# A decoder step on one core: phases that prepare the next phase's first steps, another order of the first weight pair, layer norms split in two parts, and weight splits moved to GpSimd

## Chip, cores and metric

One core of one Trainium2 chip. The metric is device time in microseconds (us) of one execution; the kernel before has a median of 2907.46 us in three runs (2906.56 to 2908.3). PE is TensorE (matmuls), DVE is VectorE, ACT is ScalarE, POOL is GpSimd, and SP is SyncE, whose queue issues most of the DMAs.

## The reference

Two layers on 1024 prompt tokens and 64 sample tokens, width 1024, all in fp32. Each sublayer is followed by a layer norm of a scaled residual:

```python
for i in range(DEPTH):                      # DEPTH = 2
    if i % 2 == 0:                          # layer 0: gated short convolution
        gb, gc, h = split(x @ w_conv_in, 3); u = gc * h
        m = (gb * conv3(u, state)) @ w_conv_out
    else:                                   # layer 1: differential attention
        q, k, v = split(x @ w_qkv, 3)       # rotated q and k; paged cache for the samples
        a = softmax(q1 k1) - lam * softmax(q2 k2)
        m = (norm(a @ v) * subln_g * (1 - lam_init)) @ w_attn_out
    x = layernorm(ALPHA * x + m, ln_mix_g[i], ln_mix_b[i])
    g, up = split(x @ w_ffn_in[i], 2)       # FFN width 2816
    x = layernorm(ALPHA * x + (silu(g) * up) @ w_ffn_out[i], ln_ffn_g[i], ln_ffn_b[i])
```

Outputs are `y` for prompt and samples, the convolution buffers and the new keys and values.

## The kernel before

Every fp32 product is made of three passes (high by high, high by low, low by high), so each operand is split: ACT copies it into a high part, DVE subtracts to get the low part (`split_to`). Of a 128x1024 weight tile these are `whi` and `wlo` (`load_split`, from `raw`).

The phases follow each other. An **in-phase** (`in_type`: convolution in, FFN in of both layers) multiplies pairs of weight blocks with the activations by Strassen's scheme: seven products for a pair of blocks instead of eight, over seven combinations `xh`, `xl` of the activations (class `Combos`), with weight combinations `ws` (class `Weights`). Products of pair n and n + 1 are interleaved in a fixed order (`order`); six are prepared ahead. The products (`pin`, L240) have two chunks of 272 columns, 12 matmuls of 272 columns in each. Results go to DRAM (`z_dram`, `h_dram`).

An **out-phase** (`out_type`: convolution out, attention out, FFN out) loads them back, and goes over the 8 prompt tiles of 128 tokens in three groups (`GROUPS`, tiles 0, 1, 4, then 2, 5, 6, then 3, 7). Within a group a step is one of 8 feature blocks (22 in the FFN): a load of 512 KB of weights (`raw`), of the group's activations (`hr`, split into `hh` and `hl`), in group 0 of the samples' (`hs`), and 6 matmuls for each tile (`pout`, L321), and two for the samples (`pouts`, L324). Two steps are prepared ahead; `hr`, `hh` and `hl` have two buffers each. After a group `ln_prompt` normalises each tile: two DVE passes with the residual `x`, the square sum on ACT, the reciprocal root on POOL (`rs_t`, `rs_r`), and two DVE passes for mean and gain (L357), and for the root and bias (L363). The tile is stored to `x_dram` and turned: `pair` transposes tiles q and q + 4 on PE and forms the seven combinations; `to_plain` transposes one tile for qkv. Turns of a group are done between the steps of the next one (`side`), those of the last group after it.

The scheduler orders the engines, except PE in the in-phases and in qkv and attention, where the program's order stands; SP's order is fixed in the attention.

Of the kernel before, what the change touches and what calls it, by code (L numbers as in the profile page):

```python
# [9 lines left out]
F32 = mybir.dt.float32  # L10
# [32 lines left out]
GROUPS = ((0, 1, 4), (2, 5, 6), (3, 7))  # L43
# [5 lines left out]
def decoder_kernel(ctx: ExitStack, tc: tile.TileContext, i_: dict, o_: dict):  # L49
# [5 lines left out]
    wsp = ctx.enter_context(tc.tile_pool(name="wsp", bufs=8))  # L55
    sml = ctx.enter_context(tc.tile_pool(name="sml", bufs=4))
    drp = ctx.enter_context(tc.tile_pool(name="drp", bufs=1, space=bass.MemoryType.DRAM))
# [4 lines left out]
    pairs = cst.tile([P, P], F32, name="pairs")  # L62
    xsT = cst.tile([P, KT, NS], F32, name="xsT")
# [15 lines left out]
    def load_split(src, width=D, eng=None, sub=None, lo_raw=False):  # L79
        raw = rawp.tile([P, width], F32, name="raw", tag="raw")  # L80
        (eng or SP).dma_start(raw, src)
        hi = wsp.tile([P, width], F32R, name="whi", tag="w")
        lp, tag = (rawp, "raw") if lo_raw else (wsp, "w")
        lo = lp.tile([P, width], F32R, name="wlo", tag=tag)
        split_to(hi, lo, raw, sub)
        return hi, lo, raw
# [17 lines left out]
    class Combos:  # L104
# [11 lines left out]
        def pair(self, psum, x1, x2, q):  # L116

            cs = slice(32 + q * P, 32 + q * P + P)

            def turned(k0):  # L120
                ps = psum.tile([P, 2, 512], F32, name="ptr", tag="b")
                for n, x in enumerate((x1, x2)):
                    for k in range(4):
                        PE.transpose(ps[:, n, k * P:k * P + P], x[:, (k0 + k) * P:(k0 + k + 1) * P], ident)
                return ps

            def v(t):
                return t.rearrange("p (k t) -> p k t", k=4)

            def scratch(name):  # L130
                return scp.tile([P, 512], F32, name=name, tag="sc")

            ps = turned(0)
            t1, t3 = scratch("t1"), scratch("t3")
            self.put(B11, cs, v(ps[:, 0, :]))
            ACT.copy(t3, ps[:, 1, :])
            DVE.tensor_tensor(t1, t3, ps[:, 0, :], op=ALU.subtract)
            ps = turned(4)
            t2 = scratch("t2")
            DVE.tensor_tensor(t2, ps[:, 1, :], t1, op=ALU.subtract)  # L140
            DVE.tensor_tensor(t3, ps[:, 1, :], t3, op=ALU.subtract)
            self.put(B21, cs, ps.rearrange("p n (k t) -> p n k t", k=4), 2)
            self.put(X1, cs, v(t1))
            self.put(X3, cs, v(t3))
            t4 = scratch("t4")
            DVE.tensor_tensor(t4, ps[:, 0, :], t2, op=ALU.subtract)
            self.put(X2, cs, v(t2))
            self.put(X4, cs, v(t4))
# [22 lines left out]
    class Weights:  # L171


        def __init__(self, src1, src2):
            self.src = src1, src2
            self.done = {}

        def raw(self, n):
            if n not in self.done:
                t = rawp.tile([P, D], F32, name="raw", tag="raw")  # L180
                SP.dma_start(t, self.src[n])
                self.done[n] = t
            return self.done[n]

        def make(self, p):
# [23 lines left out]
            split_to(w[:, 0, :], w[:, 1, :], src)  # L209
# [6 lines left out]
    def in_type(psum, x, work):  # L216


        order = [(0, 1), (0, 2)]
        for n in range(len(work)):  # L220
            order += [(n, 7), (n, 6)] + ([(n + 1, 1)] if n + 1 < len(work) else []) + [(n, 5)]
            order += ([(n + 1, 2)] if n + 1 < len(work) else []) + [(n, 4), (n, 3)]
        made, nxt = {}, 0
        banks = {}

        def prep(upto):
            nonlocal nxt
            while nxt < min(upto, len(order)):
                n, p = order[nxt]
                made[n, p] = work[n][0].make(p)  # L230
                nxt += 1

        def mm(ps, w, p, start, chunks=(0, 1)):
            for c in chunks:
                cs = slice(c * CW, c * CW + CW)
                for k in range(4):
                    ks = slice(k * P, k * P + P)
                    b = OPERAND[p]
# [4 lines left out]
        prep(6)  # L243
        with tc.manual_schedule(engines={mybir.EngineType.PE}):
            for at, (n, p) in enumerate(order):
                put = work[n][1]
                w = made.pop((n, p))
                if p in (1, 2, 7):
                    banks[n, p] = psum.tile([P, 2, 512], F32, name=f"pin{p}", tag="b")
                ps = banks[n, {1: 1, 6: 1, 5: 1, 3: 1, 7: 7, 4: 7, 2: 2}[p]]  # L250
                mm(ps, w, p, p in (1, 2, 7))
                v = ps[:, :, :CW]
                if p in (1, 6, 5):
                    ACT.copy(put.dst({1: 0, 6: 2, 5: 3}[p]), v)
                if p in (2, 5, 4):
                    blk = {2: 0, 5: 3, 4: 2}[p]
                    d = put.dst(blk)
                    DVE.tensor_tensor(d, d, banks[n, 7][:, :, :CW] if p == 5 else v, op=ALU.add)
                    put.done(blk)
                elif p == 3:  # L260
                    put.last(v)
                prep(at + 7)


    def out_type(psum, pool, nf, h_src, s_src, w_src, res, res_s, ln):

        gb = [pool.tile([P, D], F32, name=f"ln{nm}", tag=f"ln{nm}", bufs=1) for nm in "gb"]
        for t, nm in zip(gb, ("ln_g", "ln_b")):
            SP.dma_start(t, i_[nm][ln["n"]:ln["n"] + 1, :].partition_broadcast(P))
        steps = [(g, f) for g in range(len(GROUPS)) for f in range(nf)]  # L270
        made, nxt = {}, 0

        def prep(upto):
            nonlocal nxt
            while nxt < min(upto, len(steps)):
                g, f = steps[nxt]
                nxt += 1
                w = load_split(w_src[f])
                ts = GROUPS[g]
                raw = pool.tile([P, len(ts), P], F32, name="hr", tag="hr", bufs=2)  # L280
                n = 0
                while n < len(ts):
# [4 lines left out]
                    SP.dma_start(raw[:, n:m, :], h_src[f][:, c0:c0 + (m - n) * P].rearrange("p (n t) -> p n t", t=P))  # L287
                    n = m
                hh = pool.tile([P, len(ts), P], F32R, name="hh", tag="hh", bufs=2)
                hl = pool.tile([P, len(ts), P], F32R, name="hl", tag="hl", bufs=2)  # L290
                split_to(hh, hl, raw)
                hs = None
                if g == 0:
                    if s_src is None:
                        hs = pool.tile([P, 2, 32], F32, name="hs", tag="hs", bufs=2)
                        SP.dma_start(hs, h_src[f].rearrange("p (a t) -> p a t", a=2)[:, :, 0:32])
                        hs = hs.rearrange("p a t -> p (a t)")
                    else:
                        hs = s_src(f)
                made[g, f] = w, hh, hl, hs  # L300

        side = []
        kept = {}
        prep(2)
        for g, ts in enumerate(GROUPS):
            last = g == len(GROUPS) - 1
            pss = [psum.tile([P, 2, 512], F32, name="pout", tag="b") for _ in ts]
            if g == 0:
                pq = psum.tile([P, 2, 512], F32, name="pouts", tag="b")
                xs = pool.tile([P, 512], F32, name="xs", tag="xs", bufs=1)  # L310
                fold(lambda half: xs[half * NS:half * NS + NS, :], res_s)
            for t in ts:
                kept[t] = pool.tile([P, D], F32, name="x", tag="x", bufs=3)
                SP.dma_start(kept[t], res(t))
            for f in range(nf):
                (wh, wl, raw), hh, hl, hs = made.pop((g, f))
                for n, ps in enumerate(pss):
                    for hf in range(2):
                        cs = slice(hf * 512, hf * 512 + 512)
                        for m, (a, b) in enumerate(passes(hh[:, n, :], hl[:, n, :], wh[:, cs], wl[:, cs])):  # L320
                            PE.matmul(ps[:, hf, :], a, b, start=(f == 0 and m == 0), stop=(f == nf - 1 and m == 2))  # L321
                if g == 0:
                    for half in range(2):
                        PE.matmul(pq[half * NS:half * NS + NS, 0, :], hs, raw[:, half * 512:half * 512 + 512],  # L324
                                  start=(f == 0), stop=(f == nf - 1), skip_group_check=True)
                prep(g * nf + f + 3)
                if f >= 2 and side:
                    side.pop(0)()
            while side:
                side.pop(0)()  # L330
            if g == 0:
                ss = sml.tile([P, 1], F32, name="lsms", tag="lsms", bufs=2)
# [862 lines left out]
```

## Time and profile before

| | us |
|---|---|
| median of three runs | 2907.46 |
| profiled execution, whole | 2907.33 |
| its span, first to last instruction | 2905.6 |
| conv in, conv out | 34 to 291, to about 444 |
| FFN in, out (layer 0) | to 918, to about 1212 |
| qkv, attention, attention out | to 1600, to 1976, to about 2127 |
| FFN in, out (layer 1) | to about 2602, to 2894 |

The mean granted TensorE clock is 0.971. The stages' bounds are read from the first and the last matmul of each phase on the timeline. In a row of waits the engine, its output and its line stand first, then what it waited for, the total in us, the number of waits and the longest. In a row of a table by stretches stand the bounds and the length in us, then the busy time of each engine with its instructions, the granted clock, and the DMA's share. A group's row has its total and, in ns, the mean of one instruction.

### The profile page before, as it was taken

The numbers are of one execution on the slowest core, as the hardware profiler recorded it, in microseconds if no ns is written. First come the engines' busy times: TensorE is split into PE (matmuls) and PEld (weight loads), VectorE is DVE, ScalarE is ACT, GpSimd is POOL, SyncE is SP. The second block draws the span as 40 slices with busy tenths as digits, with TensorE's granted clock in tenths as the row PEclk, the third lists the DMA queues.
The fourth block names the chain that finished last, engine by engine and source line by source line (L and its number), as shares of the span: only waits on it lengthen the run. The fifth ranks groups of instructions, "written<-read, shape, count | busy, mean of one in ns | idle before, by whom it ended". The sixth has DMA issues, their size and how long they took to land.

```text
span 2905.6 us, 51121 instructions
## 1 busy us (share of the span) xinstructions
PE 2728.5 (94%) x20436; PEld 2364.7 (81%) x20436; DVE 1497.9 (52%) x2565; ACT 1043.0 (36%) x1921; POOL 253.4 (9%) x481
## 2 busy tenths in 40 slices
PE   6999879999998999899999999997889999989997
PEld 6999559999997677689888666665679999986676
DVE  7666476555552365522222666673775555532555
ACT  4222254333332244412122556562543333322343
POOL 0000010000000010111111232330100000000100
PEclk9999989999999999899999999998999999999999
DMA  3111652222223466775877888834622222234666
GB/s 123 67 60 62 199 182 81 75 82 72 79 73 118 139 212 202 228 260 200 278 275 254 287 299 309 288 110 144 211 77 80 73 82 75 75 100 147 203 190 191
DMA packets 187728, 454.95 MB, mean 157 GB/s; under 512 B 36545, under 2 KB 85330, under 8 KB 187490
## 3 DMA queue, kind: packets, MB, share of 16 engines
q1 hardware_dynamic: 175442, 408.88, 42.3%
q0 software_dynamic: 11904, 42.55, 4.3%
q8 instruction: 160, 2.62, 0.4%
q14 instruction: 78, 0.64, 0.1%
q10 hardware_dynamic: 144, 0.26, 0.0%
HBM read 387.44 MB, written 64.17 MB: 155 GB/s over the span
## 4 chain that ended last, share of the span: by engine, by line
PE 64%; issue 23%; DMA 5%; DVE 3%; ACT 2%; POOL 2%; SPq 1%; DVEq 0%; POOLq 0%; ACTq 0%
PE pin L240 25%; PE pout L321 14%; PE psqkv L930 10%; PE psS L995 3%; PE psO L833 3%; PE pso L1030 2%; PE psS L775 2%; PE psaT L1023 1%; PE pouts L324 1%; DMA raw<-wfo 1%; PE psq L717 1%; DMA hr<-h_dram 1%; DVE wlo L77 1%; PE psS L998 1%; DVE xl L77 0%
## 5 line engine op out<-in xcount | busy, mean ns | idle before, releaser
L240 PE MATMUL pin<-xh,ws 128*128 128x272 f32 x6272 | 1199.4, 290 | 39.6 <-ACT ws L76 18.6
L240 PEld LDWEIGHTS pin<-xh,ws 128*128 128x128 f32 x6272 | 1000.3, 190 | 43.4 <-ACT ws L76 19.1
L240 PE MATMUL pin<-xl,ws 128*128 128x272 f32 x3136 | 914.2, 292 | 2.2 <-DVE xl L77 2.1
L240 PEld LDWEIGHTS pin<-xl,ws 128*128 128x128 f32 x3136 | 594.6, 190 | 3.1 <-DVE xl L77 3.1
L321 PE MATMUL pout<-whi,hh 128*128 128x512 f32 x960 | 391.4, 409 | 56.6 <-ACT hh L76 43.6
L77 DVE TENSOR_TENSOR wlo<-raw,whi 128x1024 fp32r<-128x1024 f32 x204 | 250.8, 1230 | 291.0 <-ACT whi L76 260.7
L321 PE MATMUL pout<-whi,hl 128*128 128x512 f32 x960 | 381.5, 400 | 4.2 <-DVE hl L77 4.2
L321 PE MATMUL pout<-wlo,hh 128*128 128x512 f32 x960 | 381.2, 398 | 0.0
L76 ACT CAST whi<-raw 128x1024 fp32r<-128x1024 f32 x204 | 213.6, 1048 | 287.7 <-DMA raw<-wfo 145.6
L321 PEld LDWEIGHTS pout<-whi,hh 128*128 128x128 f32 x960 | 184.3, 192 | 145.9 <-ACT hh L76 69.2
L77 DVE TENSOR_TENSOR ws<-s,ws 128x512 fp32r<-128x512 f32 x224 | 154.5, 690 | 141.6 <-ACT ws L76 141.0
L930 PE MATMUL psqkv<-whi,xTh 128*128 128x256 f32 x768 | 222.6, 290 | 2.4 <-DVE xTl L77 2.4
L321 PEld LDWEIGHTS pout<-whi,hl 128*128 128x128 f32 x960 | 183.9, 192 | 49.5 <-DVE hl L77 8.0
L321 PEld LDWEIGHTS pout<-wlo,hh 128*128 128x128 f32 x960 | 184.5, 192 | 38.2 <-DVE wlo L77 0.3
L930 PE MATMUL psqkv<-wlo,xTh 128*128 128x256 f32 x768 | 214.7, 279 | 0.0
L930 PE MATMUL psqkv<-whi,xTl 128*128 128x256 f32 x768 | 214.4, 279 | 0.0
L76 ACT CAST ws<-s 128x512 fp32r<-128x512 f32 x224 | 138.8, 620 | 205.8 <-PE pin L240 103.8
L77 DVE TENSOR_TENSOR hl<-hr,hh 128x384 fp32r<-128x384 f32 (+1 forms) x180 | 94.4, 525 | 184.0 <-ACT hh L76 183.8
L76 ACT CAST hh<-hr 128x384 fp32r<-128x384 f32 (+1 forms) x180 | 85.4, 475 | 260.8 <-PE pout L321 167.1
L94 POOL TENSOR_SCALAR rs_t<-lss 128x1 f32<-128x1 f32 x32 | 22.0, 686 | 1691.9 <-ACT pout L355 1085.7
L77 DVE TENSOR_TENSOR ws<-raw,ws 128x512 fp32r<-128x512 f32 x168 | 115.4, 688 | 99.6 <-ACT ws L76 99.6
L930 PEld LDWEIGHTS psqkv<-whi,xTh 128*128 128x128 f32 x768 | 145.0, 189 | 18.0 <-issue 14.1
(219 smaller groups left out, 3269.7 us busy)
## 6 DMA issues: line engine op xcount, KB each, us to landing
raw<-wfo SPq DMA_DIRECT2D x132, 512.0 KB, 3.9
kpg<-ck SPq DMA_DIRECT2D x128, 512.0 KB, 5.3
vpg<-cv SPq DMA_DIRECT2D x128, 512.0 KB, 4.9
raw<-wfi SPq DMA_DIRECT2D x88, 512.0 KB, 3.3
h_dram<-hf SPq DMA_DIRECT2D x44, 544.0 KB, 2.7
raw<-wci SPq DMA_DIRECT2D x24, 512.0 KB, 3.3
raw<-wco SPq DMA_DIRECT2D x24, 512.0 KB, 3.8
x_dram<-x SPq DMA_DIRECT2D x24, 512.0 KB, 3.0
```

Source lines behind the costliest of these rows:

```text
L76: ACT.copy(hi, src)
L77: (eng or DVE).tensor_tensor(lo, src, fv(hi), op=ALU.subtract)
L240: PE.matmul(ps[:, c, :CW], a, y, start=(start and k == 0 and m == 0), stop=(k == 3 and m == 2), skip_group_check=True)
L321: PE.matmul(ps[:, hf, :], a, b, start=(f == 0 and m == 0), stop=(f == nf - 1 and m == 2))
L324: PE.matmul(pq[half * NS:half * NS + NS, 0, :], hs, raw[:, half * 512:half * 512 + 512], start=(f == 0), stop=(f == nf - 1), skip_group_ch ...
L717: PE.matmul(psq[half * NS:half * NS + NS, pr * 256:pr * 256 + 256], xsT[:, 4 * kh + k, :], raws[half][:, k, :], start=(kh == 0 and k == 0) ...
L775: PE.matmul(ps[32 * t:32 * t + 32, n, :], qp[:, 2 * t + h2, :], kp[:, 2 * t + h2, :], start=(h2 == 0), stop=(h2 == 1), skip_group_check=True)
L833: PE.matmul(O[32 * t:32 * t + 32, :], PT[:, p, 32 * t:32 * t + 32], vp[:, 2 * t:2 * t + 2, :].rearrange("p h d -> p (h d)"), start=(p == 0 ...
L930: PE.matmul(ps[t][:, t % 2, :256], a[:, k, t0:t0 + P], b_[:, cs], start=(k == 0 and n == 0), stop=(k == KT - 1 and n == 2), skip_group_che ...
L995: PE.matmul(svs[c][:, bk, :], a[cp, i, :], b_[cp, bk * w:bk * w + w], start=(m == 0), stop=(m == 2), skip_group_check=True)
L998: PE.matmul(svs[c][:, nb - 1, w - P:w], idb, cmask, start=False, stop=True, skip_group_check=True)
L1030: PE.matmul(po, aT[:, k, :], vn[:, k, :], start=(k == 0), stop=(k == i))
```

## The change

The in-phase and the out-phase become classes whose steps can be prepared from outside.

1. `InPhase`: the first pair runs chunk 0 of its seven products, then chunk 1. `tail` holds the last two half-turns of the phase before, done within chunk 0. When its own products are all prepared it prepares the first two steps of the out-phase (`after`), and `fill` puts two of three products of the out-phase's first step between its last products. Eight products are prepared ahead, with 7 buffers instead of 8 for the splits.
2. `OutPhase`: one `hr` buffer and one for `hs`. Groups are `PAIRED` for convolution and attention (three `hr` loads a step in groups 0 and 1), `PLAIN` for the FFN (one, two and one). In the last group the last two features of tile 0 come first, then its norm, then those of tile 1; turns begin at the fourth feature, two per step; and the FFN's first weights are prepared.
3. `ln_prompt` with `gb` None (after convolution and attention) does one DVE pass instead of two, without gain and bias. These come in at two places: in `pair`, where ACT scales each transposed 128x128 block, 16 per pair, and in the FFN's out-phase, where POOL multiplies and adds to each reloaded residual tile.
4. Low parts of the convolution's and the attention's output weights, and of the first pair of weights of convolution and of each FFN, are subtracted on POOL, 512 columns at a time.
5. `to_plain` turns in halves, and the last two turns are done in qkv's first block. The samples' transposed activations go to `a_dram`, the first two steps of the attention's out-phase are prepared before the last heads are done, and the start loads the input in smaller pieces, and the first weights by ACT's queue.

```diff
-GROUPS = ((0, 1, 4), (2, 5, 6), (3, 7))
+PAIRED = ((0, 4, 1), (5, 2, 6), (3, 7))
+PLAIN = ((0, 1, 2), (3, 4, 5), (6, 7))
...
-    wsp = ctx.enter_context(tc.tile_pool(name="wsp", bufs=8))
+    wsp = ctx.enter_context(tc.tile_pool(name="wsp", bufs=7))
@@ load_split @@
+        if sub is POOL:
+            ACT.copy(hi, raw)
+            for cs in (slice(0, width // 2), slice(width // 2, width)):
+                POOL.tensor_tensor(lo[:, cs], raw[:, cs], fv(hi[:, cs]), op=ALU.subtract)
@@ Combos.pair(self, psum, x1, x2, q, gb) @@
+                    for k in range(4):
+                        PE.transpose(ps[:, n, k * P:k * P + P], x[:, (k0 + k) * P:(k0 + k + 1) * P], ident)
+                    for k in range(4):
+                        ACT.activation(b[:, k, :], ps[:, n, k * P:k * P + P], AF.Identity,
+                                       scale=gb[:, 0, k0 + k:k0 + k + 1], bias=gb[:, 1, k0 + k:k0 + k + 1])
+            b11, b12 = turned(0)
+            self.put(B11, cs, b11)
+            DVE.tensor_tensor(b11, b12, b11, op=ALU.subtract)
+            yield
...
@@ InPhase @@
+            first = (1, 2, 7, 6, 5, 4, 3)
+            self.steps = [(0, p, (0,)) for p in first] + [(0, p, (1,)) for p in (1, 2)]
...
+        def run(self, psum, after=None, tail=(), fill=()):
...
+                    if chunks == (0,) and p in (5, 3) and tail:
+                        tail.pop(0)()
+                    if n == len(self.work) - 1 and p in (5, 4) and fill:
+                        fill.pop(0)()
+                    if self.prep(live) and after and len(self.made) <= 6:
+                        after()
@@ OutPhase @@
-                raw = pool.tile([P, len(ts), P], F32, name="hr", tag="hr", bufs=2)
+                raw = hp.tile(shape, F32, name="hr", tag="hr", bufs=1)
...
+        def more(self, ahead=2):
+            if self.nxt < ahead:
+                self.prep(self.nxt + 1)
...
+        def fill(self, psum, n):
+            def go():
+                self.early[n] = psum.tile([P, 2, 512], F32, name="pout", tag="b")
+                self.products(self.early[n], 0, 0, n)
+            return go
...
+                for t in ts:
+                    kept[t] = pool.tile([P, D], F32, name="x", tag="x", bufs=4)
+                    SP.dma_start(kept[t], res(t))
+                    if gb:
+                        POOL.tensor_tensor(kept[t], kept[t], gb[ln["n"] - 1][0], op=ALU.mult)
+                        POOL.tensor_tensor(kept[t], kept[t], gb[ln["n"] - 1][1], op=ALU.add)
+                late = 2 if last else 0
+                wait = 3 if last else 1
+                for f in range(nf - late):
...
+                    self.prep(g * nf + f + 3)
+                    if last and after and f >= nf - 6:
+                        after()
+                    for _ in range(2 if last else 1):
+                        if f >= wait and side:
+                            side.pop(0)()
...
+                for n, t in enumerate(ts):
+                    for f in range(nf - late, nf):
+                        self.products(pss[n], g, f, n)
+                    ln_prompt(kept[t], pss[n], t, gb.get(ln["n"]), ln)
@@ ln_prompt @@
+        if gb is None:
+            DVE.tensor_scalar(x, x, nmu[:, 0:1], r[:, 0:1], op0=ALU.add, op1=ALU.mult)
+            SP.dma_start(ln["keep"](t), x)
+            return
@@ FeedForward @@
+        def first(self):
+            self.into.prep(min(len(self.into.made) + 1, 5))
...
+        def run(self, psum, tail):
+            self.into.run(psum, self.out.more, tail, [self.out.fill(psum, n) for n in range(2)])
@@ qkv, attention @@
+                            if first and t % 2 and late:
+                                late.pop(0)(psb, "pb")
...
+        wao.prep(2)
         for x in todo:
```

On PE, at the end of the convolution's in-phase, the out-phase's first matmuls followed the last product (`pin` is a product of the in-phase, `pout` of the out-phase). Before:

```order
L240 MATMUL pin_2650<-xh,ws 128x272 x2
L240 MATMUL pin_2650<-xl,ws 128x272
L240 MATMUL pin_2650<-xh,ws 128x272
L321 MATMUL pout<-whi,hh 128x512
L321 MATMUL pout<-wlo,hh 128x512
```

Now, some way ahead of the last product:

```order
L260 MATMUL pin_2722<-xl,ws 128x272
L260 MATMUL pin_2722<-xh,ws 128x272
L345 MATMUL pout<-whi,hh 128x512
L345 MATMUL pout<-wlo,hh 128x512
L345 MATMUL pout<-whi,hl 128x512
L345 MATMUL pout<-whi,hh 128x512
L345 MATMUL pout<-wlo,hh 128x512
L345 MATMUL pout<-whi,hl 128x512
L345 MATMUL pout<-whi,hh 128x512
L260 MATMUL pin_2924<-xh,ws 128x272
L260 MATMUL pin_2924<-xl,ws 128x272
```

Seven `pout` matmuls of the first step stand between two in-products, and six more behind the second of these.

On SP, where the FFN of layer 0 goes from its in-phase to its out-phase (`ev` is the last in-result, `raw` weights, `x` and `xs` residual tiles). Before:

```order
L461 DMA h_dram_21_104<-hf 128x1088
L269 DMA lnb<-ln_b 128x1024
L287 DMA hr<-h_dram_0_83 128x256
L287 DMA hr<-h_dram_0_83 128x128
L296 DMA hs<-h_dram_0_83 128x2x32
L287 DMA hr<-h_dram_1_84 128x256
L287 DMA hr<-h_dram_1_84 128x128
```

Now, where the `hr` rows of steps 0 to 2 stand far ahead:

```order
L359 DMA lng_9097<-ln_g 128x1024
L536 DMA h_dram_21_106<-ev 128x544
L332 DMA hs<-h_dram_1_86 128x2x32
L359 DMA lnb_9098<-ln_b 128x1024
L359 DMA lng_9101<-ln_g 128x1024
L359 DMA lnb_9102<-ln_b 128x1024
L109 DMA xs<-s_dram_161 64x512 x2
L372 DMA x<-x_dram_0_137 128x1024
L372 DMA x<-x_dram_1_138 128x1024
L372 DMA x<-x_dram_2_139 128x1024
L332 DMA hs<-h_dram_2_87 128x2x32
L84 DMA raw<-wfo 128x1024
```

The last row is the weights of step 3; two gain and bias tiles have joined what stands ahead of it.

On POOL, in the last group of the convolution's out-phase there were the norms' rows alone (`rs_t`, `rs_r`). Now:

```order
L91 TENSOR_TENSOR wlo<-raw,whi 128x512 x2
L102 TENSOR_SCALAR rs_t<-lss 128x1
L104 TENSOR_TENSOR rs_r<-rs_t,mhalf 128x1
L91 TENSOR_TENSOR wlo<-raw,whi 128x512 x2
L80 TENSOR_TENSOR ws<-raw,ws 128x512
L91 TENSOR_TENSOR wlo<-raw,whi 128x512 x2
L80 TENSOR_TENSOR ws<-raw,ws 128x512
L91 TENSOR_TENSOR wlo<-raw,whi 128x512 x2
L80 TENSOR_TENSOR ws<-s_4032,ws 128x512
L91 TENSOR_TENSOR wlo<-raw,whi 128x512 x2
L80 TENSOR_TENSOR ws<-s_4122,ws 128x512
L80 TENSOR_TENSOR ws<-s_4121,ws 128x512
```

The low parts of the output weights (`wlo`) and of the FFN's first weights (`ws`) now stand between the norms' rows, in POOL's one queue.

More of the change, by code (lines that the diff above doesn't have):

```diff
@@ L241, in mm @@
                                   stop=(k == 3 and m == 2), skip_group_check=True)
[L243 to L262, printed above, removed]
@@ L265, in out_type @@
[L265 to L279, printed above, removed]
-                raw = pool.tile([P, len(ts), P], F32, name="hr", tag="hr", bufs=2)
+        def run(self, psum, after=None, tail=(), fill=()):
+            tail, fill = list(tail), list(fill)
+            assert len(tail) in (0, 2)
+            live = 8
+            self.prep(live)
+            with tc.manual_schedule(engines={mybir.EngineType.PE}):
+                for at, (n, p, chunks) in enumerate(self.steps):
+                    put = self.work[n][1]
+                    w = self.made[n, p]
+                    if chunks != (0,):
+                        del self.made[n, p]
+                    role = self.ROLE[p]
+                    if p == role and chunks != (1,):
+                        self.banks[n, role] = psum.tile([P, 2, 512], F32, name=f"pin{p}", tag="b")
+                    ps = self.banks[n, role]
+                    self.products(ps, w, p, chunks)
+                    c = slice(chunks[0], chunks[-1] + 1)
+                    v = ps[:, c, :CW]
+                    if p in (1, 6, 5):
+                        ACT.copy(put.dst({1: 0, 6: 2, 5: 3}[p])[:, c], v)
+                    if p in (2, 5, 4):
+                        blk = {2: 0, 5: 3, 4: 2}[p]
+                        d = put.dst(blk)[:, c]
+                        DVE.tensor_tensor(d, d, self.banks[n, 7][:, c, :CW] if p == 5 else v, op=ALU.add)
+                        if chunks != (0,):
+                            put.done(blk)
+                    elif p == 3 and chunks != (0,):
+                        put.last(ps[:, :, :CW])
+                    if chunks == (0,) and p in (5, 3) and tail:
[4 more added lines that the diff above has]
+                        after()
@@ L300, in prep @@
[L300 to L321, printed above, removed]
-                if g == 0:
[L323 to L332, printed above, removed]
-                DVE.scalar_tensor_tensor(xs, xs, ALPHA, pq[:, 0, :], op0=ALU.mult, op1=ALU.add, accum_out=ss)
-                it = ln_sample(psum, xs, ss, ln)
-                next(it)
-                side += [lambda it=it: next(it, None)] * 5
-            for n, t in enumerate(ts):
-                ln_prompt(kept[t], pss[n], t, gb, ln)
-            for t in ts:
-                side += [lambda th=th: th() for th in ln["turn"](t, kept)]
-            if last:
-                while side:
-                    side.pop(0)()
@@ L381, in ln_sample @@
         ps = psum.tile([P, 2, 512], F32, name="pln", tag="b")
[L382 removed]
+        halves(ps[:, 0, 0:1], ss)
         t = sml.tile([P, 1], F32, name="lts", tag="lts", bufs=2)
@@ L517, in flat @@
+                work = []
                 def flat(t):
@@ L627, in decoder_kernel @@
         xTl = xtp_pool.tile([P, KT, NT], F32R, name="xTl")
-        keep, keeps = kept_in(1)
-        ffn_out(0, psum, 0, norm(1, to_plain(psum, xTh, xTl), plain_sample(xTh, xTl), keep, keeps))
-    scs.close()
+        with tc.tile_pool(name="fo0", bufs=2, reuse_waits="tile") as pool:
+            keep, keeps = kept_in(1)
+            late = ff.out.run(psum, pool, *kept_in(0),
+                              norm(1, to_plain(psum, xTh, xTl), plain_sample(xTh, xTl, xsT), keep, keeps))
+    ap3s = ExitStack()
     with tc.tile_pool(name="kvp", bufs=1, reuse_waits="tile") as kvp, \
@@ L1077, in decoder_kernel @@
                     turned = next(turn)
+        step(200)
+        for h in range(NH):
+            POOL.dma_start(a_dram[h].rearrange("p (a t) -> p a t", a=2)[:, :, 0:32],
+                           xsT[:, h, :].rearrange("p (a t) -> p a t", a=2))
+        wao.prep(2)
         for x in todo:
```

385 lines of the change are left out of this document (239 added, 146 removed).

## The prediction

> **What bounds the kernel now.** I read the page's first part, then what TensorE (PE) waited for, then a table of stretches.
>
> ```profile
> span 2905.6 us, 51121 instructions
> PE 2728.5 (94%) x20436; PEld 2364.7 (81%) x20436; DVE 1497.9 (52%) x2565; ACT 1043.0 (36%) x1921; POOL 253.4 (9%) x481
> ```
>
> PE is busy for 94% of the span and every other engine has room, so PE sets the time, and at most 2905.6 - 2728.5 = 177 us of idle time, plus the time in which PE runs slowly, can go without removing work. The change removes next to no matmuls. The profiled run took 2907.33 us, 1.7 more than its span; the median of the three runs is 2907.46, so one sum serves for both. About 0.2%, 6 us, is what a measurement of this kernel can tell from no change.
>
> ```profile
> PE pout L321 <- ACT hh L76: 43.6, 6, 10.9
> PE ptr L124 <- DVE x L363: 21.0, 4, 8.2
> PE pin L240 <- ACT ws L76: 18.6, 3, 17.0
> PE pin L240 <- DVE ws L77: 12.1, 4, 8.5
> PE ptr L414 <- DVE x L363: 11.3, 3, 6.4
> PE pout L321 <- DVE t L146: 10.1, 2, 5.0
> PE ptr L124 <- DVE t L137: 9.4, 4, 4.3
> ```
>
> Columns: total us, times, longest. These 26 waits hold 126 of the 177 us, and all are at seams: `hh` is the first operand of an out-phase, `x` the layer norm's end before the turns, `t` the turns' combinations, `ws` an in-phase's first weights. The next table cuts the span around those seams.
>
> ```profile
> core 0: us, PE busy (x) PEld busy (x) DVE busy (x) ACT busy (x) POOL busy (x), PEclk, DMA share, GB/s
> 290.80:340.00 49.20, 38.33 (x150) 25.77 (x149) 10.87 (x14) 8.84 (x13) 0.00 (x0) 0.86 0.58 183
> 340.00:375.00 35.00, 34.13 (x150) 25.91 (x150) 27.01 (x42) 16.65 (x25) 9.67 (x11) 1.00 0.70 219
> 375.00:450.00 75.00, 49.81 (x231) 40.16 (x229) 59.77 (x101) 36.62 (x63) 7.92 (x10) 0.82 0.47 159
> 910.00:950.00 40.00, 31.24 (x136) 23.41 (x136) 7.47 (x11) 5.76 (x10) 0.00 (x0) 0.83 0.52 166
> ...
> 1190.00:1240.00 50.00, 36.84 (x207) 32.55 (x206) 26.58 (x52) 19.16 (x25) 7.69 (x12) 0.83 0.66 210
> 1960.00:2010.00 50.00, 33.57 (x128) 22.80 (x127) 11.77 (x20) 12.65 (x28) 6.76 (x14) 0.73 0.39 129
> ...
> 2055.00:2135.00 80.00, 55.26 (x248) 44.40 (x246) 61.60 (x103) 37.78 (x66) 11.30 (x11) 0.83 0.47 155
> 2595.00:2640.00 45.00, 35.17 (x160) 25.26 (x161) 9.64 (x14) 8.00 (x12) 0.00 (x0) 0.89 0.52 163
> ```
>
> Idle time is the stretch less PE's busy time; in steady work (340 to 375) the granted clock is 1.00 and little is idle. After a gap the clock is low, and the same matmuls take longer:
>
> ```profile
> 301.99 6.86 PE pout L321 x18
> ...
> 320.55 4.33 PE pout L321 x18
> 324.88 1.01 PE pouts L324 x4
> ```
>
> So a seam costs its idle time plus about (1 - clock) of its busy time. Conv in to conv out: 10.9 + 2.5 (6.86 - 4.33) = 13.4. The turns before the first FFN: 25.2 + 0.18 x 49.8 = 34. FFN in to out, layer 0: 8.8 + 0.17 x 31.2 = 14. To qkv: 13.2 + 0.17 x 36.8 = 19.5. Attention to its projection: 16.4 + 9 = 25.5. The turns before the second FFN: 24.7 + 9.4 = 34. FFN in to out, layer 1: 9.8 + 3.9 = 13.7. Sum **154 us** at seven seams.
>
> **The change, part by part.** *Fill and early preparation (conv in to out).* Two steps of the out-phase are now prepared before the in-phase ends, and two of the first step's three products stand between the last in-products. The 10.9 us chain (last store, `hr` load, `hh`) is then needed only by the steps of the last two features. Of 13.4 I take **12** as gone (bounds 8 and 13.4: all but one slow restart, 2.5, and a load of 3.0, quoted below; or all).
>
> *Turns before the FFNs.* New: two of the three pairs of group 2 are turned beside its matmuls, the last pair inside chunk 0, which is 7 products of 12 matmuls. What it costs the other engines, from these rows:
>
> ```profile
> L77 DVE TENSOR_TENSOR wlo<-raw,whi 128x1024 fp32r<-128x1024 f32 x204 | 250.8, 1230 | 291.0 <-ACT whi L76 260.7 <-PE pin L240 14.8 <-PE psqkv L930 14.0
> L77 DVE TENSOR_TENSOR hl<-hr,hh 128x256 fp32r<-128x256 f32 x60 | 25.0, 419 | 13.7 <-ACT hh L76 13.7
> L77 DVE TENSOR_TENSOR xl<-t,xh 128x512 fp32r<-128x512 f32 x32 | 21.7, 683 | 3.1 <-ACT xh L76 2.9
> ...
> L1006 ACT ACTIVATE pexp<-psS,pnm 128x128 f32<-128x128 f32 x16 | 5.7, 362 | 8.9 <-DVE pnm L1002 8.9
> ```
>
> ```profile
> 369.33 1.24 DVE L77 TENSOR_TENSOR wlo<-raw,whi 128x1024 fp32r<-128x1024 f32 x1 [1.01 <-ACT whi L76]
> 370.49 1.66 DVE L77 TENSOR_TENSOR hl<-hr,hh 128x384 fp32r<-128x384 f32 x1
> ...
> 374.31 0.56 DVE L77 TENSOR_TENSOR hl<-hr,hh 128x384 fp32r<-128x384 f32 x1 [1.03 <-ACT hh L76]
> ```
>
> ```profile
> 369.56 2.17 POOL L388 TENSOR_TENSOR xs<-xs,gbf 128x512 f32<-128x512 f32 x1
> ```
>
> A pair now costs ACT 16 activations of 128x128, 16 x 0.36 = 5.8 us, and 7 casts (4.8, at DVE's 0.68), 21 for two pairs with 8 `whi` casts apart; just inside PE's group, which lasts 8 x 12/18 x 4.33 + 3.5 for transposes = 26.6. DVE has 11 operations per pair, 11 x 0.68 = 7.5, 15 for two, and 8 x 0.42 for `hl`: 18.4. POOL gets 16 half-row `wlo` operations and five `ws`. No row has that form; the nearest are 0.68 (DVE's own) and the last one quoted, 2.17, so 21 cost 14 to 46 us. The rows show more: POOL's began at 369.56 while DVE's `wlo` ran to 370.57, and `hl` ended at 372.15, 0.42 after POOL's. So POOL's own time is about 2.17 - 1.0 = 1.2, 25 us for 21, and while it ran, `hl` stood still. If the two engines ran freely side by side, 25 would fit into 26.6, and some 4 us would remain for the last pair. Standing still for each other they need 18.4 + 25 = 43, and 17 of the 34 remain, 18 with the last pair. I take the second: gain **16** at each of the two places (bounds 30: free; -3: POOL at 2.17). The shorter norm (one pass for two) is in the residue. In groups 0 and 1 the same splits on POOL, 2.4 us a step, lie beside 4.3 us of matmuls and cost nothing.
>
> The Trainium skill's page "SBUF — State Buffer", section "Who interferes with whom", states that a DVE instruction with two SBUF inputs and a GpSimd instruction that reads SBUF exclude each other for whole instructions. By that rule this term is the 16 above, without it 30; the rows at 370 us agree with it (1.66 for 0.56), and it speaks against moving splits to GpSimd while DVE turns pairs.
>
> *FFN in to out.* Filled in the same way, worth up to 14. But SyncE's queue now has four gain and bias tiles, `xs` and three residual tiles ahead of the weights of step 3, and the first of them waits for PE's last in-product, since the pool reuses the operands' memory. That is 7 x 512 KB + 128 KB + 512 KB of weights, 4.2 MB; at the 200 GB/s or so of the busy stretches 21 us, plus 2.3 for `whi` and `wlo`. PE has step 0's third product and two whole steps, 1.4 + 3 x 1.0 + 8.7 = 13, ahead of it. A new wait of 5 to 10 us per layer takes most of the gain: **4** each (bounds -3 and 12).
>
> *Out-phases with one `hr` buffer.* It was two. The last column is us from issue to landing:
>
> ```profile
> hr<-h_dram SPq DMA_DIRECT2D x88, 128.0 KB, 3.0
> ...
> hs<-h_dram SPq DMA_DIRECT2D x44, 32.0 KB, 2.3
> ```
>
> A load can start only when `hl` of the step before is done: 0.4 issue + 2.3 to 3.0 + 0.42 each for `hh` and `hl` = 3.5 to 4.2 us a step. PE's step is 2.9 (12/18 of 4.33) in the last group and 4.3 in the others. So the first two groups lose nothing; the last group of an FFN loses 0.6 x 20 = 12 at the short landing, less 5.8 that two prepared steps cover: **-7** in layer 0, **-5** in layer 1, where the last group no longer begins behind a norm (bounds 0, as the load may be early anyway, and 1.3 x 20 - 5.8 = -20, each). In the 8-step phases the lead covers it. POOL's 16 reload multiplies and adds per FFN (each twice L388's size, 2.4) I cost at nothing: matmuls hide them; uncovered they are 38 per FFN.
>
> *To qkv.* The last two turns move into qkv's first block, so PE needn't wait for the second norm: half of 19.5, **10** (bounds 3 and 16: the wait for `x` (11.3 in three) and its restarts). *Attention to projection:*
>
> ```profile
> 1985.25 0.79 PE L321 MATMUL pout<-whi,hh 128*128 128x512 f32 x1 [10.51 <-ACT hh L76]
> ```
>
> Seven of eight features don't need the last head and are now prepared before it is done, so this wait and its restart go: 10.5 + 2.5 = **13** (bounds 6 and 18).
>
> *Start and end.* The start gives **0**: PE's first chunk needs half the weights, but its sixth product waits for an evacuation that shares a buffer with the second chunk's input, and DVE has 44 half-size operations for 22 full ones, 22 x (2 x 0.68 - 1.23) = 3 more. Bounds -3 and 5 (7 half-size splits less ahead of PE). The end, where tile 6's norm now runs under tile 7's last matmuls, **2** (0 and 4).
>
> Sum: 12 + 16 + 16 + 4 + 4 - 7 - 5 + 10 + 13 + 0 + 2 = 65. 2907.3 - 65 = **2842 us**.
>
> **The rivals.** *A: all seams close.* If the two engines hardly meet and the weights of step 3 come in time: 154 less 4 to 5 a seam (one short restart), 120 gone, out-phases at no loss: **2787**. For it: every long wait named above is answered by an edit. Against it: the 370 us rows.
>
> *B: slower, the single `hr` buffer binds.* Its price is decided by where a load lies behind 512 KB of weights in the queues:
>
> ```profile
> 1188.41 4.82 DMA raw<-wfo
> ...
> 1196.77 4.82 DMA raw<-wfo
> ```
>
> The chain of waits in the last group already runs through weight loads every 8.4 us for three buffers, 2.8 a step, as long as PE's step. If `hr` lands in 4.8 like these, a step is 0.4 + 4.8 + 0.8 = 6.0: last groups lose 3.1 x 20 - 5.8 = 56 in each FFN, 112 in both, against 65 + 12 gained elsewhere: **2942**. It is level with before when the last groups cost 38 each, at a cycle of 5.1 us. Against it: a load-bound `hr` comes after its weights have landed, not behind them.
>
> *C: the lock reaches into the FFN out-phases.* The 32 reload operations hold a DVE split back by 1.1 (1.66 less 0.56) each in steps where DVE is just in time, and PE waits: 32 x 1.1 = 35: **2877**. The same skill section would have it so, and says that order of issue decides who blocks; no run here shows a 1024-wide GpSimd operation beside them.
>
> *D: the change doesn't do what it says:* the early preparations wait for buffers (7 split buffers for 8), and seams stay: 2905.
>
> **How the numbers follow.** Forecast 0.50, A 0.17, C 0.18, B 0.08, D 0.07. The range covers forecast, C and most of A, and widens at the slow end for the `hr` bounds (13 to 15 more in each FFN): 2782 to 2888. Faster is forecast, A and C, 0.85; same is most of D, 0.06; slower is B and a rest of D, 0.09.
>
> **What would show it.** Right: the waits of `pout` for `hh` fall from 43.6 to under 15; both turn stretches keep 15 to 20 us idle and slow, PE waiting there for `xl`, `ws` or `hl` with POOL busy; a wait for `whi` or `wlo` three steps into the FFN out-phases; steps of 3.4 to 3.6 us in their last groups, released by `hh`. Wrong: those steps at 2.8 or above 5; turn stretches without idle time; a long gap at the start; waits inside qkv.

## The result, and the profile after

The changed kernel takes 3059.89 us (median of four runs, 3053.22 to 3069.52) against 2907.22 before: a ratio of 1.0527, with a 95% interval of 1.0492 to 1.0563. It is 153 us slower, where 65 us less were forecast. The page of its profiled execution:

```profile
span 3064.3 us, 51378 instructions
...
PE 2787.6 (91%) x20468; PEld 2372.9 (77%) x20468; DVE 1490.7 (49%) x2527; ACT 1095.6 (36%) x2080; POOL 506.7 (17%) x638
```

PE's busy time rose by 59 us with only 32 more matmuls. Some 36 of the 59 us stand in the `pout` matmuls, of which there are as many as before: those of `whi` and `hh`, `whi` and `hl`, `wlo` and `hh` took 391, 382 and 381 us and now take 408, 390 and 393, with a lower granted clock in the stretches below. PE's idle time rose from 177 to 277 us. What it waited for (total, times, longest):

```profile
PE pout L345 <- ACT hh L79: 106.0, 82, 4.4
PE pout L345 <- DVE hl L80: 30.6, 29, 3.9
PE pin L260 <- ACT gc L284: 12.4, 2, 11.9
PE ptr L134 <- ACT xb L136: 11.2, 8, 1.7
...
PE pouts L385 <- DMA hs<-h_dram: 8.8, 3, 4.1
```

The wait for `hh` was six long waits at seams, 43.6 us. Now it is 82 short ones, 106 us: it has moved from the seams into the steps of the out-phases, and grown. By stretches, first two groups and last group of the FFN out-phase of layer 0, from the last product of the in-phase and divided at the last group's first matmul, before:

```profile
918.00:1142.30 224.30, 215.06 (x912) 156.34 (x913) 98.61 (x125) 74.86 (x102) 9.06 (x11) 0.98 0.61 186
1142.30:1208.00 65.70, 64.10 (x289) 51.80 (x287) 46.20 (x66) 34.70 (x50) 6.44 (x9) 1.00 0.73 228
```

and after:

```profile
936.60:1190.80 254.20, 224.38 (x908) 156.69 (x907) 113.71 (x127) 74.33 (x103) 46.87 (x25) 0.95 0.53 165
1190.80:1298.80 108.00, 74.51 (x289) 51.85 (x287) 53.09 (x68) 36.71 (x56) 16.46 (x13) 0.95 0.45 150
```

(length, PE busy, weight loads, DVE, ACT, POOL, clock, DMA share, GB/s.) Nearly the same matmuls take 30 us longer in the first two groups and 42 in the last. A step in the last group, on ACT (start, duration, tile, and the idle time before with its releaser):

```profile
1268.77 1.04 ACT L79 CAST whi<-raw 128x1024 fp32r<-128x1024 f32 x1 [3.13 <-PE pout L345]
1269.72 0.40 ACT L79 CAST hh<-hr 128x256 fp32r<-128x256 f32 x1
1273.26 1.04 ACT L79 CAST whi<-raw 128x1024 fp32r<-128x1024 f32 x1 [3.14 <-PE pout L345]
1274.21 0.40 ACT L79 CAST hh<-hr 128x256 fp32r<-128x256 f32 x1
```

on SP, and on PE:

```profile
1266.12 0.33 SPq L323 DMA_DIRECT2D hr<-h_dram  x1
1269.79 0.33 SPq L84 DMA_DIRECT2D raw<-wfo  x1
1270.61 0.33 SPq L323 DMA_DIRECT2D hr<-h_dram  x1
```

```profile
1270.17 0.51 PE L345 MATMUL pout<-whi,hh 128*128 128x512 f32 x1 [1.44 <-ACT hh L79]
1274.66 0.50 PE L345 MATMUL pout<-whi,hh 128*128 128x512 f32 x1 [1.44 <-ACT hh L79]
```

The loads of `hr` in this stretch, with their size and the time from issue to landing:

```profile
hr<-h_dram SPq DMA_DIRECT2D x2, 128.0 KB, 3.0
```

A step takes 4.49 us (1270.17 to 1274.66), of which PE waits 1.44. Two loops run here. One is the forecast's: `hr` issued 1266.12, landed 3.0 later at about 1269.1, cast as `hh`, then `hl`, then the next `hr` at 1270.61. It has some 0.6 us to spare, since `hh` begins only at 1269.72. The other goes through PE: the step's end frees a split buffer, ACT starts `whi`, and `hh`, which PE waits for, stands behind `whi` in ACT's queue. Its links fill the step: 0.95 from `whi` to `hh` (1268.77 to 1269.72), 0.45 to the first matmul, and 3.09 from there to the next `whi` (1273.26).

### The profile page after: what moved, and what is told of

It reads as the page before. It is cut to its first block, busy times and chain, and to the rows that moved or that the text cites. A ratio compares the mean times of both kernels' runs of the same rounds, so it can differ in the third digit from the quotient of the medians.

```text
span 3064.3 us, 51378 instructions
## 1 busy us (share of the span) xinstructions
PE 2787.6 (91%) x20468; PEld 2372.9 (77%) x20468; DVE 1490.7 (49%) x2527; ACT 1095.6 (36%) x2080; POOL 506.7 (17%) x638
## 5 line engine op out<-in xcount | busy, mean ns | idle before, releaser
L345 PE MATMUL pout<-whi,hh 128*128 128x512 f32 x960 | 408.1, 426 | 109.6 <-ACT hh L79 106.0
L345 PE MATMUL pout<-whi,hl 128*128 128x512 f32 x960 | 389.6, 417 | 30.9 <-DVE hl L80 30.6
L345 PE MATMUL pout<-wlo,hh 128*128 128x512 f32 x960 | 392.9, 410 | 7.1 <-DVE wlo L80 7.1
L80 DVE TENSOR_TENSOR wlo<-raw,whi 128x1024 fp32r<-128x1024 f32 x156 | 211.5, 1357 | 337.5 <-ACT whi L79 163.1
L79 ACT CAST whi<-raw 128x1024 fp32r<-128x1024 f32 x156 | 163.5, 1048 | 405.5 <-DMA raw<-wfo 197.3
L80 DVE TENSOR_TENSOR ws<-s,ws 128x512 fp32r<-128x512 f32 x212 | 146.3, 690 | 262.8 <-ACT ws L79 262.8
L80 DVE TENSOR_TENSOR hl<-hr,hh 128x384 fp32r<-128x384 f32 (+1 forms) x180 | 125.5, 697 | 205.6 <-ACT hh L79 187.9
L374 POOL TENSOR_TENSOR x<-x,lng 128x1024 f32<-128x1024 f32 x16 | 41.9, 2621 | 1032.5 <-DMA x<-x_dram 995.6
L79 ACT CAST ws<-raw 128x512 fp32r<-128x512 f32 x168 | 104.2, 621 | 294.9 <-PE pin L260 203.5
L91 POOL TENSOR_TENSOR wlo<-raw,whi 128x512 fp32r<-128x512 f32 x96 | 131.5, 1392 | 153.5 <-ACT whi L89 95.7
```

The costliest lines, as they stand in the source:

```text
L79: ACT.copy(hi, src)
L80: (eng or DVE).tensor_tensor(lo, src, fv(hi), op=ALU.subtract)
L91: POOL.tensor_tensor(lo[:, cs], raw[:, cs], fv(hi[:, cs]), op=ALU.subtract)
L374: POOL.tensor_tensor(kept[t], kept[t], gb[ln["n"] - 1][0], op=ALU.mult)
```

## The experiments

Two theories: H, the single `hr` buffer; L, GpSimd and DVE standing still for each other. Ratios are to runs of the kernel before on the same chip, with their 95% interval.

**1. Two `hr` buffers.**

```diff
-raw = hp.tile(shape, F32, name="hr", tag="hr", bufs=1)
+raw = hp.tile(shape, F32, name="hr", tag="hr", bufs=2)
```

> The changed kernel with two buffers for `hr` again, nothing else. Theory H (the single buffer makes load, `hh`, `hl` and the next load one chain, whose load lies behind 512 KB of weights): most of the loss goes, 80 to 130 us faster than the changed kernel, 2930 to 2980 us, and a step of the last group of an FFN out-phase falls from 4.5 to under 3.1 us. Theory L (GpSimd and DVE standing still for each other): less than 30 us faster, over 3030.

2916.67 us, ratio 1.0032 (1.002 to 1.0045): 143 us faster than the changed kernel, more than the 80 to 130 that H gave. The same two stretches:

```profile
917.40:1141.50 224.10, 215.01 (x907) 154.58 (x906) 113.98 (x128) 73.61 (x104) 47.09 (x25) 0.97 0.59 187
1141.50:1209.50 68.00, 65.60 (x289) 52.73 (x287) 50.32 (x68) 36.15 (x55) 13.91 (x12) 0.97 0.67 224
```

30 us come back in the first two groups and 40 in the last. On ACT in the last group:

```profile
1180.00 0.41 ACT L79 CAST hh<-hr 128x256 fp32r<-128x256 f32 x1 [1.34 <-DMA hr<-h_dram]
1180.31 1.04 ACT L79 CAST whi<-raw 128x1024 fp32r<-128x1024 f32 x1
1182.34 0.41 ACT L79 CAST hh<-hr 128x256 fp32r<-128x256 f32 x1 [0.99 <-DMA hr<-h_dram]
1182.65 1.05 ACT L79 CAST whi<-raw 128x1024 fp32r<-128x1024 f32 x1
1185.25 0.41 ACT L79 CAST hh<-hr 128x256 fp32r<-128x256 f32 x1 [1.55 <-DMA hr<-h_dram]
```

Now `hh` waits for its load and no longer behind a `whi` that waits for PE, and steps come every 2.3 to 2.9 us. The order of ACT's queue, which the scheduler writes, is another too. Counted from the phase's first casts, the `whi` at 1268.77 in the changed kernel is that of step 64 and the `hh` behind it that of step 61; here the `hh` of step 57 (1180.00) stands ahead of the `whi` of step 58. So the edit gives back a buffer and, with it, this order, and what each alone is worth was not separated. What remains is 10 us slower than before: without its worst part the change gains nothing.

**2. All splits on DVE, one `hr` buffer.**

```diff
-out = OutPhase(KT, z_dram, i_["wco"], PAIRED, POOL)
+out = OutPhase(KT, z_dram, i_["wco"], PAIRED)
...
-wao = OutPhase(KT, a_dram, i_["wao"], PAIRED, POOL)
+wao = OutPhase(KT, a_dram, i_["wao"], PAIRED)
...
-                                              sub=POOL if f == 0 else None), Put(f)) for f in range(FT)])
+                                              sub=None), Put(f)) for f in range(FT)])
```

> The changed kernel with the low parts of weights subtracted on DVE again, one `hr` buffer. Theory H: within 15 us of the changed kernel (3045 to 3075), the FFN out-phases unchanged, as they had no split on GpSimd. Theory L: 40 us or more faster (under 3020), in the stretches of the convolution's and the attention's out-phases and turns.

3027.53 us, ratio 1.0415 (1.039 to 1.044): 32 us faster, between the two (H at most 15, L at least 40).

**3. No gain and bias on reloaded tiles, one `hr` buffer.**

```diff
-                    if gb:
-                        POOL.tensor_tensor(kept[t], kept[t], gb[ln["n"] - 1][0], op=ALU.mult)
-                        POOL.tensor_tensor(kept[t], kept[t], gb[ln["n"] - 1][1], op=ALU.add)
```

> The changed kernel without the gain and bias on the reloaded residual tiles (32 GpSimd operations of 128x1024 left out; the output lacks them). Theory H: within 15 us of the changed kernel. Theory L for the FFN out-phases: 30 us or more faster, in their first two groups.

The output lacks the gain and bias. 3033.55 us in one run, 26 us faster: again between the two. So L has a part too.

**4. The kernel before with one `hr` buffer.**

```diff
-raw = pool.tile([P, len(ts), P], F32, name="hr", tag="hr", bufs=2)
+raw = pool.tile([P, len(ts), P], F32, name="hr", tag="hr", bufs=1)
```

> The kernel before with one `hr` buffer in place of two, nothing else. Theory H: 60 to 130 us slower than before (2967 to 3037), in the out-phases, steps of about 4.5 us in the last groups. Theory L: within 20 us of before.

3099.13 us in one run, 192 us slower than before: the one edit costs more than the whole change, and more than the 60 to 130 of H. On ACT in its last group:

```profile
1285.55 0.41 ACT L76 CAST hh<-hr 128x256 fp32r<-128x256 f32 x1 [1.10 <-DMA hr<-h_dram]
...
1290.42 0.41 ACT L76 CAST hh<-hr 128x256 fp32r<-128x256 f32 x1 [0.53 <-DMA hr<-h_dram]
```

These two casts are 4.87 us apart, and both waited for their load. At other steps of this group `hh` stands right behind a `whi` that waited for PE, as in the changed kernel; on average a step takes 5.7 us (124.8 us for 22).

**5. Two `hr` buffers and all splits on DVE** (1 and 2 together).

> The changed kernel with two `hr` buffers and all low parts of weights subtracted on DVE again. If GpSimd and DVE stand still for each other at the turns (theory L, beside H), 15 to 35 us faster than with two `hr` buffers alone (2880 to 2902), in conv out, attention out and their turns; if moving the splits cost nothing once the loads are early, within 6 us of it (2911 to 2923).

2898.41 us, ratio 0.9971 (0.9958 to 0.9983): 18 us faster than experiment 1, as L gives. Rows by operation; the turns' low parts (total, mean in ns of one) in experiment 1:

```profile
L80 DVE TENSOR_TENSOR xl<-xb,xh 128x512 fp32r<-128x512 f32 x56 | 49.0, 890 | 20.4 <-ACT xh L79 19.9
```

and here:

```profile
L80 DVE TENSOR_TENSOR xl<-xb,xh 128x512 fp32r<-128x512 f32 x56 | 37.5, 686 | 11.2 <-ACT xh L79 10.8
...
L424 DVE TENSOR_SCALAR x<-x,nmu,rs_r 128x1024 f32<-128x1024 f32 x16 | 13.0, 814 | 11.5 <-POOL rs_r L104 10.1 <-ACT whi L79 0.7 <-ACT hh L79 0.7
```

Each low part takes 204 ns less where GpSimd has no splits. The second row, the shorter norm's pass, is read at the end.

**6. The `hr` load ahead of the weight load, one buffer.** The line `w = load_split(...)` of `prep` stands behind the `hr` loads.

> The changed kernel with one `hr` buffer, and the `hr` load issued ahead of the step's weight load instead of behind it. If the load's place behind 512 KB of weights makes the cycle long, a last group's step falls from 4.5 to about 3.6 us (0.4 + 2.1 to 2.3 + 0.8) and the kernel to 2990 to 3030; if the chain through one buffer is long in itself, it stays within 15 us of the changed kernel.

3075.02 us in one run: 15 us slower, neither of the two. ACT in its last group:

```profile
1254.47 1.04 ACT L79 CAST whi<-raw 128x1024 fp32r<-128x1024 f32 x1 [3.11 <-PE pout L345]
1255.42 0.40 ACT L79 CAST hh<-hr 128x256 fp32r<-128x256 f32 x1
1258.95 1.04 ACT L79 CAST whi<-raw 128x1024 fp32r<-128x1024 f32 x1 [3.13 <-PE pout L345]
1259.90 0.40 ACT L79 CAST hh<-hr 128x256 fp32r<-128x256 f32 x1
1264.76 0.40 ACT L79 CAST hh<-hr 128x256 fp32r<-128x256 f32 x1 [4.46 <-DMA hr<-h_dram]
```

Most steps of the group are like the first two shown: 4.48 us, with `hh` right behind a `whi` that waited for PE. A few, like the last, wait for their load. So the place behind 512 KB of weights isn't what makes the step long. What the load's loop would take without the other stays open; an eighth split buffer, which would loosen the loop through PE, was not tried.

**7. Half of the block operations on DVE** (on experiment 5).

```diff
+                        if n == 0:
                             ACT.activation(b[:, k, :], ps[:, n, k * P:k * P + P], AF.Identity, ...)
+                        else:
+                            DVE.tensor_scalar(b[:, k, :], ps[:, n, k * P:k * P + P], gb[:, 0, k0 + k:k0 + k + 1],
+                                              gb[:, 1, k0 + k:k0 + k + 1], op0=ALU.mult, op1=ALU.add)
```

> The kernel with two `hr` buffers and splits on DVE, and half of the turns' 16 block operations (gain and bias from PSUM) on DVE instead of ACT. If ACT's 16 activations per pair bind the turns (transposes waited 25 us for `xb` in the first experiment), 8 to 20 us faster than the same kernel without it; if DVE binds, the same or slower.

2904.26 us, ratio 0.9994 (0.9985 to 1.0004): 6 us slower. ACT isn't what binds the turns once the splits are on DVE.

**8. The convolution's first pair in whole products** (on experiment 5).

```diff
-conv = InPhase(xc, work)
+conv = InPhase(xc, work, False)
...
+                self.steps = [(0, p, (0, 1)) for p in (1, 2)]
+                self.order = [(0, 1), (0, 2)]
```

> The kernel with two `hr` buffers and splits on DVE, and the convolution's first pair in whole products again instead of chunk by chunk (the FFNs' stay by chunk). If the evacuation that waits for the second chunk's input (a wait of 12 us in the changed kernel) costs what it shows, 5 to 10 us faster than without; if the earlier first matmul pays for it, the same or slower.

2894.34 us, ratio 0.9966 (0.9951 to 0.9981): the intervals of this and experiment 5 overlap, so no difference is shown.

**9. Two `hs` buffers** (on experiment 8): `bufs=1` of `hs` to `bufs=2`.

> The kernel with two `hr` buffers, splits on DVE and the convolution's first pair whole, and now two buffers for `hs` as before the change. PE waited 9 us in three waits for `hs` at the start of the FFN out-phases; if the second buffer lets those loads start ahead of the gain and residual tiles, 5 to 12 us faster than without it (2882 to 2889); if the weights behind the same loads are as late, within 4 us.

2891.96 us, ratio 0.9939 (0.9922 to 0.9955): 8 us by the ratios, but the intervals just overlap.

**10. Experiment 9 without the reloaded tiles' gain and bias** (experiment 3's edit).

> The same without the gain and bias on the reloaded residual tiles (the output lacks them). The 26 us that this gave with one `hr` buffer: if GpSimd's 32 operations hold back DVE as such, 15 to 35 us faster again; if they only lengthened the single-buffer chain, under 8 us.

The output lacks them again. 2869.79 us, ratio 0.9863 (0.9843 to 0.9882): 22 us faster than experiment 9, so the 26 us of experiment 3 were no matter of the single buffer.

**11. The FFN's first pair's splits on GpSimd again** (on experiment 9).

> As e9, with the FFN's first pair's low parts on GpSimd again (convolution's and attention's output weights stay on DVE). PE waits 7 us at each FFN in-phase for the last tile's square, whose sum DVE starts late, behind those splits. If DVE's queue is the limit there, 4 to 12 us faster than e9; if the standing still of the two engines costs as much, the same.

2889.94 us, ratio 0.9933 (0.9916 to 0.9949): the same.

**12. Gain and bias of reloaded tiles on DVE** (on experiment 9; `POOL.tensor_tensor` becomes `DVE.tensor_tensor`).

> As e9, with the reloaded tiles' gain and bias on DVE instead of GpSimd (32 operations of about 1.25 us). If GpSimd's operations held DVE for their whole length (2.6 us each beside it), 5 to 25 us faster than e9; if DVE's own time in the out-phases is short, slower by up to 20.

2883.0 us, ratio 0.9908 (0.9891 to 0.9925): 9 us faster than experiment 9 on the same chip (2880.33 to 2885.42 against 2890.08 to 2893.34), and faster than both kernels. The operation was this, in the changed kernel:

```profile
L374 POOL TENSOR_TENSOR x<-x,lng 128x1024 f32<-128x1024 f32 x16 | 41.9, 2621 | 1032.5 <-DMA x<-x_dram 995.6
```

and DVE's split of the 3-tile activations had a mean of 792 ns in the changed kernel; in experiment 9 and here it was:

```profile
L80 DVE TENSOR_TENSOR hl<-hr,hh 128x384 fp32r<-128x384 f32 x120 | 87.8, 732 | 52.3 <-ACT hh L79 41.8 <-DMA x<-x_dram 10.5
...
L80 DVE TENSOR_TENSOR hl<-hr,hh 128x384 fp32r<-128x384 f32 x120 | 70.3, 586 | 55.8 <-ACT hh L79 55.4 <-issue 0.4
```

Before the change it was 578. The seams of experiment 12, stretch by stretch:

```profile
286.00:336.00 50.00, 50.00 (x233) 34.92 (x232) 20.19 (x33) 13.18 (x18) 0.62 (x2) 1.00 0.56 177
360.00:436.00 76.00, 56.25 (x268) 45.29 (x267) 57.87 (x108) 56.45 (x123) 4.87 (x10) 0.89 0.52 176
885.00:935.00 50.00, 43.76 (x220) 31.59 (x218) 20.79 (x22) 9.69 (x13) 0.00 (x0) 0.93 0.52 168
1180.00:1235.00 55.00, 41.50 (x256) 35.37 (x255) 22.77 (x51) 15.20 (x23) 7.37 (x13) 0.88 0.51 177
1945.00:1995.00 50.00, 41.11 (x170) 28.19 (x169) 15.53 (x28) 16.18 (x38) 15.54 (x27) 0.80 0.52 156
2045.00:2125.00 80.00, 57.58 (x302) 47.39 (x301) 59.51 (x107) 60.97 (x130) 5.20 (x10) 0.91 0.42 142
2560.00:2605.00 45.00, 39.52 (x215) 30.23 (x214) 19.25 (x21) 10.25 (x14) 0.00 (x0) 0.99 0.54 182
```

and two of its waits:

```profile
PE pin L264 <- ACT pout L425: 14.3, 2, 7.2
...
PE psq L839 <- DMA raws<-wqkv: 7.0, 2, 6.8
```

## Why the prediction was wrong

**The step that failed: "Out-phases with one `hr` buffer".** It put -7 and -5 on the edit; experiment 1 puts 143 us on it, and experiment 4 shows a cost of the same order in the kernel before. The single buffer was named, as a term and as rival B (2942 us, 8%), and both were wrong in three ways.

First, the cycle was a sum of a load and two casts, 3.5 to 4.2, and the term took its short end, with the 2.3 us of the 32 KB loads. In the last group the load took 3.0, and that loop alone would come to some 3.9, an estimate (3.0, then 0.9 from the start of `hh` at 1269.72 to the next issue at 1270.61). The step was 4.49: it was held by the loop through PE, `whi` and `hh`, which the term didn't have, because it added durations and didn't ask what stands ahead of `hh` in ACT's queue. How much of the 143 us is that order and how much the missing buffer by itself stays open. The last groups, by their first and last matmuls, get back 40 us in layer 0 and 27 in layer 1 from experiment 1.

Second, the term held that PE's 4.3 us a step hide the cycle in the first two groups: 30 us were lost there in layer 0 and 10 in layer 1. Third, "in the 8-step phases the lead covers it": experiment 1 gives back 19 us in conv out and the FFN in behind it, and 24 in the attention's. Together these are 150 us, the difference of the two profiled spans (3064.3 and 2914.8). The range's bound of -20 for each FFN counted one loop and no queue. Of the signs, the waits for `hh` were to fall under 15 us and rose to 106, and last-group steps of 3.4 to 3.6 us took 4.49, between the two values that were named as wrong.

**The GpSimd terms.** The turns' estimate took the standing still of the two engines into account and priced it at 14 us for each place (16 gained where 30 would be free), 28 in all. Measured, the splits on GpSimd cost 18 us in all (experiments 1 and 5), 32 with the single buffer. The reload operations, costed at nothing because matmuls hide them, cost 22 us (experiment 10), of which 9 come back on DVE (experiment 12). That was rival C, 35 us, and its mechanism shows in the rows of `hl`: 732 ns with these operations on GpSimd (experiment 9), 586 with them on DVE (experiment 12).

**The seams** in experiment 12, by the forecast's own reckoning (idle time plus slow clock), against before: conv in to out 0 from 13.4, where 12 were forecast to go; the two turns 26 and 28 from 34, 8 and 6 gained, where 16 each were forecast, though with splits on GpSimd; FFN in to out 9 from 14 and 6 from 13.7, 5 and 8 for 4 each; to qkv 18.5 from 19.5, 1 for 10; attention to projection 17 from 25.5, 8.5 for 13. So the fill and the early steps did what they say. At the turns and at qkv the old wait went and a new one came, which the last two rows show in part: the in-phase's first chunk waits 7 us for the last tile's square, which still holds a PSUM buffer, and qkv's sample products for their weights. The terms didn't ask which tile still held a PSUM buffer. In all 50 us go at the seams of experiment 12, which is 27 faster than before; why the other 23 are given back was not found. By first and last matmuls, much of it stands in the FFN out-phases: from the last in-product to their own end they take 290 us in both layers, where 290 and 292 were taken before, though their seams are shorter and 3.3 us of their matmuls now come earlier, as the fill.

**Start.** Zero was forecast, with bounds of -3 and 5. The first product now comes at 10.6 us instead of 17.0 (the 34 in the table of stages isn't the first matmul), but the convolution's last ends at 302.0 instead of 291.1, 3.3 of which is the fill: 7.6 us lost, outside the bounds. The named wait came, 11.9 us for an evacuation (`gc`) that shares a buffer with the input. Experiment 8 takes it away; its last in-product ends at 295.4 where experiment 5's ends at 297.8, and the gain can't be told in the whole time. At the end 2 were forecast, and the span of experiment 12 still ends 12 us after its last matmul, as before.

## What to carry to other kernels

A buffer count is not a detail of memory: with one buffer, every link of load, cast and use becomes a chain, and its length is the links plus their waits in each engine's queue (here `hh` behind `whi`), so read off which instruction stands ahead of each link before adding durations. Work hidden by the bound engine can still cost if it holds back an engine that feeds it. When a change has one large new cost, undo that part first: the same rework, with two buffers for `hr` and `hs`, its splits and gains on DVE and the convolution's first pair whole, is 0.9% faster than before instead of 5.3% slower.

## What the runs showed that was not expected

DVE's standing still beside GpSimd reached a DVE pass with one tensor input too: the shorter norm's `tensor_scalar` (128x1024) took 1327 ns on average in experiment 1 and 814 in experiment 5, where no split runs on GpSimd:

```profile
L424 DVE TENSOR_SCALAR x<-x,nmu,rs_r 128x1024 f32<-128x1024 f32 x16 | 21.2, 1327 | 20.2 <-POOL rs_r L104 14.8 <-ACT whi L89 5.4
```

The Trainium skill's page "SBUF — State Buffer", section "Who interferes with whom", has both cases: a DVE instruction with two SBUF inputs, and `tensor_scalar`, which can enter a mode that takes the ports shared with GpSimd. The trace agrees in both (890 against 686 ns, 1327 against 814); which mode the pass ran in no run here shows. And one ACT operation on a 128x128 block from PSUM with scale and bias took 0.46 us, not the 0.36 of the row that the forecast used.
